# Full-height score products in an attention stage, and a GEMM stage's sums, differences and low halves moved from GpSimd to VectorE

## The chip, the cores and the metric

The kernel runs on one core of a Trainium2 chip. The metric is the device time of one execution, in microseconds (us); less is better. The core's engines run side by side, each through its own list of instructions in a fixed order: TensorE (PE in the profile; PEld is its weight loading), VectorE (DVE), ScalarE (ACT), GpSimd (POOL) and SyncE (SP), which issues most of the DMAs. An engine whose next instruction waits holds up everything behind it in its list.

## The reference, cut to what matters

One step of a one-layer encoder over 1,152 rows of 1,024 features (1,024 prompt rows and 8 times 16 sample rows). Three branches (a state space S5, a pooling branch, a cross-attention into 256 memory tokens) are gated, merged and multiplied by `w_out`; a residual and a gated feed-forward block follow.

```python
def memory_attention(q, mk, mv):                       # 4 heads of 64
    s = jnp.einsum('blhd,bmhd->bhlm', qh, mk) * (MEM_HEAD_DIM ** -0.5)
    p = jax.nn.softmax(s, axis=-1)
    o = jnp.einsum('bhlm,bmhd->blhd', p, mv)
...
    x = x + rmsnorm(merged @ p['w_out'], p['g_post1'])
    h2 = rmsnorm(x, p['g_pre2'])
    x = x + rmsnorm(ConvFFN(h2), p['g_post2'])         # up: 1024 -> 2 x 2816, down: 2816 -> 1024
```

## The kernel before, in words

Every large product is made in three passes from operands that are split into a high and a low part (`split`: ScalarE rounds the high part to fp32r, another engine subtracts it from the source; lines 63 and 64). `mm3` (lines 103, 106, 107) issues the three matmuls of one k-tile: high by high, high by low, low by high. The 1,152 rows lie in three chunks of 384 columns. The order of the instructions on each engine comes from a scheduler that works ahead of time from the code and a model of its own; `keep_in_program_order`, `issue_after` and `high_priority` pin a few of them.

**The attention** (lines 775 to 846, in phase 1). Queries, keys and values of the prompt come back from DRAM and are split into three tiles: `a0` holds the high queries (columns 0 to 2047) and the high and low keys, `a1` the low queries and, in four of its partitions, the negated row maxima `mT`, `a2` the values and the exponentials. Two heads share the 128 partitions: head `e` of a pair has partitions 64e to 64e+63. A first pass (line 811) makes scores from the high parts alone, rows by tokens, for the row maxima. A second pass (lines 835 to 838) makes the scores as tokens by rows: for each of 16 tiles (two row groups, two head pairs, two heads, two token halves) three products over 64 partitions and one over 4 partitions (`sel` by `mT`), which subtracts the maximum, each 512 columns wide. ScalarE takes the exponential (line 839), line 842 multiplies by the values, and VectorE divides (lines 843 and 844). Between these matmuls the scheduler lays the products of the gates (lines 103 to 107 with `hhi`, `hlo`), so TensorE has other work all through this stage.

**The output GEMM** (`phase_o`, lines 1023 to 1188). For chunk c and feature tile f, `out(c, f)` is 24 matmuls; ScalarE evacuates it (line 1078) and squares it (line 1053), and GpSimd adds the square to the chunk's sum `ssa` (line 1057). `sums` multiplies these sums by ones (line 1065, up to 18 matmuls of one column) for a root mean square, whose power runs on GpSimd (line 86); ScalarE makes three diagonal tiles of it (line 94), and TensorE spreads it over all rows (line 96). `resid` then scales the chunk, adds x (lines 1095 and 1099 on VectorE) and squares again, and `norm` scales for the second norm (line 1117). The steps of chunk c-1 are laid between the products of chunk c. At the end chunks 0 and 1 are combined for seven block products in place of eight (a Strassen scheme): VectorE and GpSimd form the blocks (lines 1153 and 1160 to 1165) and their splits (`bB..`, `bT..`). The feed-forward weights of the first two feature tiles (ff 0 and 1) are combined likewise in `up_w`: sums and differences S1 to S4 from lines 1232 to 1238, then their splits. `prods` issues the block products: for ff 0 the order is 1, 2, the sums of chunk 2, 6, 5, its `resid`, 7, 3, 4; for ff 1 it is 1, 2, the second sums of chunk 2, 6, 5, its `norm`, 7, 3, 4.

Buffers that set the order here: `w1` has six tiles and `w2` four, which hold first the split weights of the output GEMM and then those of `up_w`. So the high part of a new weight (line 63) waits until TensorE is done with the product that read the buffer.

Of the kernel before, what the change touches and what calls it, by code (L numbers as in the profile page):

```python
# [32 lines left out]
class K:  # L33
# [741 lines left out]
    def attention(self, P, pools):  # L775


        nc = self.nc
# [4 lines left out]
        Kh = a0[:, 2048:2560].rearrange("p (h m) -> p h m", h=2)  # L783
        Kl = a0[:, 2560:3072].rearrange("p (h m) -> p h m", h=2)
# [4 lines left out]
        self.split(Kh, Kl, r)  # L789
# [11 lines left out]
        sel = P.tile([4, 4, 128], F32R, tag="tg", name="sel")  # L801
        nc.vector.tensor_copy(sel, self.ident[0:4, 0:4, None].to_broadcast([4, 4, 128]))

        mx = P.tile([128, 8, 2, 2], F32, tag="mx", name="mx")
        mT = a1[0:4, 2048:3072].rearrange("p (j k) -> p j k", j=8)
        for j in range(8):
            sc = [self.sm().rearrange("p (h m) -> p h m", h=2) for _ in range(2)]
            for e in range(2):
                es = slice(64 * e, 64 * e + 64)
                for hp in range(2):  # L810
                    nc.tensor.matmul(sc[e][:, hp, :], Qh[es, hp, j, :], Kh[es, hp, :], start=True, stop=True)
                nc.vector.tensor_reduce(mx[:, j, e, :], sc[e], axis=AX.X, op=OP.max)
            if j == 3:
                next(dec)
        for g in range(2):
            t = self.sm()
            for j in range(4):
                nc.tensor.transpose(t[0:4, j * 128:j * 128 + 128], mx[:, 4 * g + j].rearrange("p e h -> p (e h)"), self.ident)
            nc.scalar.activation(mT[:, 4 * g:4 * g + 4], t[0:4].rearrange("p (j k) -> p j k", j=4), AF.Copy, scale=-1.0)
# [3 lines left out]
        for g in range(2):  # L823
            gs = slice(4 * g, 4 * g + 4)
            for hp in range(2):
                yt = P.tile([128, 4, 128], F32, tag="tmp", name="yt")
                yf = yt.rearrange("p j k -> p (j k)")
                for e in range(2):
                    es, zs = slice(64 * e, 64 * e + 64), slice(64 - 64 * e, 128 - 64 * e)
                    pT = a2[:, 1024 + 1024 * (n % 2):2048 + 1024 * (n % 2)].rearrange("p (m l) -> p m l", m=2)  # L830
                    n += 1
                    for m in range(2):
                        s = self.sm()
                        ms = slice(128 * m, 128 * m + 128)
                        nc.tensor.matmul(s, Kh[es, hp, ms], Qh[es, hp, gs], start=True, stop=False)
                        nc.tensor.matmul(s, Kh[es, hp, ms], Ql[es, hp, gs], start=False, stop=False)
                        nc.tensor.matmul(s, Kl[es, hp, ms], Qh[es, hp, gs], start=False, stop=False)
                        nc.tensor.matmul(s, sel[:, 2 * e + hp, :], mT[:, gs], start=False, stop=True)
                        nc.scalar.activation(pT[:, m, :], s, AF.Exp, scale=0.125)
                    o = self.sm()  # L840
                    for m in range(2):
                        nc.tensor.matmul(o, va[:, m, 2 * hp + e, :], pT[:, m, :], start=m == 0, stop=m == 1)  # L842
                    nc.vector.reciprocal(yf[es], o[zs])
                    nc.vector.tensor_mul(yf[es], o[es], yf[es])
# [178 lines left out]
    def phase_o(self):  # L1023
# [6 lines left out]
        if True:  # L1030
# [16 lines left out]
            def sumsq(f, src, ss, last=8):  # L1047
# [3 lines left out]
                else:  # L1051
# [4 lines left out]
                    else:  # L1056
                        self.sqadd = G.tensor_add(ss[0], ss[0], sq)  # L1057
# [74 lines left out]
            for c in range(3):  # L1132
                ss.append(ssa())
                for f in range(8):
# [4 lines left out]
                    if c:  # L1139
# [7 lines left out]
                        elif f == NF[c] + 1:  # L1147
                            with tc.high_priority():
                                norm(c - 1, rs)
                            if c == 1:  # L1150
                                op("B11", h0[:, lo])
                                op("B21", h0[:, up])
                                G.tensor_sub(h0[:, up], h0[:, up], h0[:, lo])
# [11 lines left out]
            G.tensor_sub(h0[:, up], h0[:, up], h1[:, lo])  # L1165
            op("T3", h1[:, lo], G)
            op("T4", h0[:, up], G)
# [12 lines left out]
            with tc.issue_after(self.diag.ins):  # L1180
                self.up_w(s1, (None, G, G, G))
# [32 lines left out]
    def up_w(self, s, eng=(None,) * 4):  # L1214

        G = self.nc.gpsimd
# [620 lines left out]
```

## Time and profile before

| | before |
|---|---|
| median of 3 runs | 1626.8 us (1624.13 to 1631.04) |
| the profiled execution's own time | 1622.7 us |
| its span, first to last instruction | 1620.9 us |
| TensorE busy in the span | 1558.3 us |
| VectorE, ScalarE, GpSimd busy | 1031.3, 586.2, 586.3 us |
| mean granted TensorE clock | 0.979 |

The span runs from the first to the last instruction; 1.8 us of the execution's time lie around it. Rows of the timeline read: start, duration, engine, line, operation, output<-input, partitions*columns of the weights, partitions x columns of the streamed operand, count, and in brackets the idle time before it with the engine that ended it. Ends of matmuls are modelled, so the distance from one start to the next says what a matmul costs. A row that merges several ("x3") gives the time of all of them.

### The profile page before, as it was taken

What the parts mean: (1) busy time and instruction counts of PE and PEld (TensorE: products, weight loads), DVE (VectorE), ACT (ScalarE), POOL (GpSimd) and SP (SyncE); (2) the same over time, 40 slices, a digit from 0 to 9 for tenths busy, and PEclk for the clock granted to TensorE, in tenths of its full rate; (3) what the DMA queues carried; (4) which work ended last, traced back from release to release, by engine and by line L of the source; (5) the groups of instructions that cost most, each with busy time, mean ns of one, the idle gap of its engine ahead of it and who ended that gap; (6) DMA issues with size and microseconds to landing.
All of it is one profiled execution on the core that took longest, in us unless ns stands there. A gap on an engine that the chain in (4) does not pass through costs nothing.

```text
span 1620.9 us, 22934 instructions
## 1 busy us (share of the span) xinstructions
PE 1558.3 (96%) x8964; PEld 1511.3 (93%) x8964; DVE 1031.3 (64%) x1549; ACT 586.2 (36%) x893; POOL 586.3 (36%) x509
## 2 busy tenths in 40 slices
PE   6899999999999999999879999999999999999996
PEld 5899999868899999998879999999999998999996
DVE  7864987645643354624678655555655658788866
ACT  6322444253321242434445333433333333332321
POOL 2400001000011143326666444534443426655546
PEclk9899999999999999999879999999999999999998
DMA  6343334413232235122323221212121233133214
GB/s 245 100 146 95 107 114 145 150 64 121 95 117 81 71 80 162 56 96 76 122 88 129 76 75 62 82 69 81 54 82 69 82 135 122 51 110 103 91 64 166
DMA packets 98460, 163.44 MB, mean 101 GB/s; under 512 B 23216, under 2 KB 68656, under 8 KB 98352
## 3 DMA queue, kind: packets, MB, share of 16 engines
q1 hardware_dynamic: 97920, 161.75, 30.3%
q8 instruction: 70, 1.15, 0.3%
q14 instruction: 38, 0.31, 0.1%
q10 hardware_dynamic: 432, 0.23, 0.0%
HBM read 119.52 MB, written 42.42 MB: 100 GB/s over the span
## 4 chain that ended last, share of the span: by engine, by line
PE 79%; DVE 9%; issue 3%; DMA 3%; ACT 2%; POOL 1%; POOLq 0%; SPq 0%; DVEq 0%; ACTq 0%
PE pc L107 14%; PE pc L103 14%; PE pc L106 14%; PE ps L103 10%; PE ps L106 10%; PE ps L107 10%; PE ps L842 1%; DVE dB L64 1%; DMA Ts<-DG 1%; POOL ssa L1057 1%; DVE wlo L64 1%; PE ps L1065 1%; DMA DG<-gs 1%; DMA dwr<-in_w_down 1%; DVE mg L1095 1%
## 5 line engine op out<-in xcount | busy, mean ns | idle before, releaser
L103 PE MATMUL pc<-hhi,whi 128*128 128x384 f32 x760 | 259.9, 342 | 7.7 <-ACT hhi L126 7.6
L106 PE MATMUL pc<-hlo,whi 128*128 128x384 f32 x760 | 260.7, 343 | 2.6 <-DVE hlo L127 2.6
L107 PE MATMUL pc<-hhi,wlo 128*128 128x384 f32 x760 | 257.7, 339 | 0.5 <-DVE wlo L64 0.5
L63 ACT ACTIVATE whi<-rawt 128x1024 fp32r<-128x1024 f32 x102 | 107.5, 1055 | 180.7 <-PE pc L106 80.7
L64 DVE TENSOR_TENSOR wlo<-rawt,whi 128x1024 fp32r<-128x1024 f32 x102 | 131.9, 1295 | 56.9 <-ACT whi L63 56.3
L103 PEld LDWEIGHTS pc<-hhi,whi 128*128 128x128 f32 x760 | 144.8, 191 | 10.3 <-ACT hhi L126 7.6
L106 PEld LDWEIGHTS pc<-hlo,whi 128*128 128x128 f32 x760 | 144.7, 190 | 7.4 <-DVE hlo L127 3.5
L107 PEld LDWEIGHTS pc<-hhi,wlo 128*128 128x128 f32 x760 | 144.6, 190 | 3.2 <-issue 1.6
L200 DVE TENSOR_TENSOR sg<-pc,rb 128x384 f32<-128x384 f32 x95 | 52.3, 553 | 122.7 <-PE pc L107 120.2
L107 PE MATMUL pc<-h2hi,wlo 128*128 128x384 f32 x352 | 119.1, 338 | 2.1 <-DVE wlo L64 2.0
L103 PE MATMUL pc<-h2hi,whi 128*128 128x384 f32 x352 | 118.3, 336 | 0.0
L106 PE MATMUL pc<-h2lo,whi 128*128 128x384 f32 x352 | 118.2, 336 | 0.0
L64 DVE TENSOR_TENSOR S<-S,S 128x512 fp32r<-128x512 f32 x85 | 75.9, 895 | 64.2 <-ACT S L63 62.2
L63 ACT ACTIVATE S<-S 128x512 fp32r<-128x512 f32 x88 | 55.1, 629 | 160.2 <-PE ps L107 89.8
L917 ACT ACTIVATE sg<-sg,vec 128x384 f32<-128x384 f32 x72 | 44.1, 613 | 148.2 <-DVE sg L200 121.2
L1004 POOL TENSOR_TENSOR mg<-mg,sgl 128x384 f32<-128x384 f32 x24 | 28.2, 1174 | 171.9 <-DVE sgl L1002 168.6
L103 PE MATMUL ps<-bT,S 128*128 128x384 f32 x240 | 80.2, 334 | 0.0
L106 PE MATMUL ps<-bT,S 128*128 128x384 f32 x240 | 80.2, 334 | 0.0
L107 PE MATMUL ps<-bT,S 128*128 128x384 f32 x240 | 80.2, 334 | 0.0
L1237 POOL TENSOR_TENSOR S<-rawt 128x512 f32<-128x512 f32 x22 | 29.8, 1355 | 125.9 <-PE ps L107 124.3
L63 ACT ACTIVATE dhi<-dwr 128x1024 fp32r<-128x1024 f32 x38 | 39.7, 1058 | 95.9 <-PE pc L106 61.4
L107 PEld LDWEIGHTS pc<-h2hi,wlo 128*128 128x128 f32 x352 | 66.1, 188 | 2.8 <-DVE wlo L64 2.8
(458 smaller groups left out, 4401.0 us busy)
## 6 DMA issues: line engine op xcount, KB each, us to landing
rawt<-in_w_up SPq DMA_DIRECT2D x48, 512.0 KB, 3.3
Dact<-t SPq DMA_DIRECT2D x22, 576.0 KB, 3.5
rawt<-in_w_gate SPq DMA_DIRECT2D x24, 512.0 KB, 3.5
dwr<-in_w_down SPq DMA_DIRECT2D x22, 512.0 KB, 3.5
Dsg<-sg SPq DMA_DIRECT2D x45, 192.0 KB, 1.9
sgl<-Dsg SPq DMA_DIRECT2D x45, 192.0 KB, 2.4
dBr<-Dact SPq DMA_DIRECT2D x8, 768.0 KB, 5.7
xT<-in_xT SPq DMA_DIRECT2D x12, 384.0 KB, 7.6
```

The source lines that it names most:

```text
L63: nc.scalar.activation(hi, src, AF.Copy)
L64: (eng or nc.vector).tensor_sub(lo, src, hi)
L103: i = nc.tensor.matmul(out, whi, xhi, start=start, stop=False)
L106: nc.tensor.matmul(out, whi, xlo, start=False, stop=False)
L107: nc.tensor.matmul(out, wlo, xhi, start=False, stop=stop)
L200: self.nc.vector.tensor_mul(sg, b, self.rb[:, c, :])
L842: nc.tensor.matmul(o, va[:, m, 2 * hp + e, :], pT[:, m, :], start=m == 0, stop=m == 1)
L917: self.nc.scalar.activation(sg, sg, AF.Sigmoid, bias=self.vec[:, V_BGATE + m:V_BGATE + m + 1])
L1004: nc.gpsimd.tensor_add(m, m, sp)
L1057: self.sqadd = G.tensor_add(ss[0], ss[0], sq)
L1065: m = nc.tensor.matmul(s3[:, t:t + 1], s[:, t * 128:t * 128 + 128], self.ones[:, 0:1], start=(i, t) == (0, 0), stop=(i, t) == (len(ss) - 1 ...
L1237: G.tensor_sub(s3, a11, a21)
```

## The change

In the attention the keys of each head get a tile of their own over all 128 partitions, with zeros in the other head's half (`Kh` and `Kl` with an index `e`; two memsets of 128x1024 on GpSimd, and the split in two halves of 64 partitions). The second pass then multiplies over 128 partitions; the queries of the other head meet zeros. `mT` becomes a tile of its own of 128 partitions, cleared once, and `sel` gets 128 partitions. The first pass still works on 64 partitions. In `phase_o` the additions of squares, the two block differences that GpSimd made, the low halves of T3 and T4, and in `up_w`, for ff 0 and 1, the sums and differences and the low halves of S2 to S4 go to VectorE. For ff 2 and above `up_w` is as before.

```diff
--- before.py
+++ after.py
@@ -775,18 +775,23 @@
     def attention(self, P, pools):


         nc = self.nc
         a0, a1 = [self.mtile([128, 3072], F32R, f"at{i}") for i in range(2)]
         a2 = self.mtile([128, 3072], F32, "at2")
         Qh = a0[:, 0:2048].rearrange("p (h j k) -> p h j k", h=2, j=8)
         Ql = a1[:, 0:2048].rearrange("p (h j k) -> p h j k", h=2, j=8)
-        Kh = a0[:, 2048:2560].rearrange("p (h m) -> p h m", h=2)
-        Kl = a0[:, 2560:3072].rearrange("p (h m) -> p h m", h=2)
+        Kh = a0[:, 2048:3072].rearrange("p (e h m) -> p e h m", e=2, h=2)
+        Kl = a1[:, 2048:3072].rearrange("p (e h m) -> p e h m", e=2, h=2)
         va = a2[:, 0:1024].rearrange("p (m h d) -> p m h d", m=2, h=4)
         dec = self.attention_decode(P)
         r = P.tile([128, 2, 256], F32, tag="tmp", name="kr")
         nc.sync.dma_start(r, self.O["mk"])
-        self.split(Kh, Kl, r)
+        nc.gpsimd.memset(a0[:, 2048:3072].bitcast(F32), 0.0)
+        nc.gpsimd.memset(a1[:, 2048:3072].bitcast(F32), 0.0)
+        for e in range(2):
+            es = slice(64 * e, 64 * e + 64)
+            self.split(Kh[es, e], Kl[es, e], r[es])
         for hp in range(2):
             r = P.tile([128, 8, 128], F32, tag="U", name="qr")
             nc.sync.dma_start(r, self.Dq[hp].rearrange("p (j k) -> p j k", j=8)[:, :, 0:128])
@@ -798,25 +803,27 @@
         vh = va.rearrange("p m (a e) d -> p m a e d", e=2)
         for e in range(2):
             nc.gpsimd.tensor_copy(vh[:, :, :, e, 64 * e:64 * e + 64], r[:, :, :, e, :])
-        sel = P.tile([4, 4, 128], F32R, tag="tg", name="sel")
-        nc.vector.tensor_copy(sel, self.ident[0:4, 0:4, None].to_broadcast([4, 4, 128]))
+        sel = P.tile([128, 4, 128], F32R, tag="tg", name="sel")
+        nc.vector.tensor_copy(sel, self.ident[:, 0:4, None].to_broadcast([128, 4, 128]))

         mx = P.tile([128, 8, 2, 2], F32, tag="mx", name="mx")
-        mT = a1[0:4, 2048:3072].rearrange("p (j k) -> p j k", j=8)
         for j in range(8):
             sc = [self.sm().rearrange("p (h m) -> p h m", h=2) for _ in range(2)]
             for e in range(2):
                 es = slice(64 * e, 64 * e + 64)
                 for hp in range(2):
-                    nc.tensor.matmul(sc[e][:, hp, :], Qh[es, hp, j, :], Kh[es, hp, :], start=True, stop=True)
+                    nc.tensor.matmul(sc[e][:, hp, :], Qh[es, hp, j, :], Kh[es, e, hp, :], start=True, stop=True)
                 nc.vector.tensor_reduce(mx[:, j, e, :], sc[e], axis=AX.X, op=OP.max)
             if j == 3:
                 next(dec)
+        mTt = P.tile([128, 1024], F32R, tag="CA", name="mT")
+        nc.gpsimd.memset(mTt.bitcast(F32), 0.0)
+        mT = mTt.rearrange("p (j k) -> p j k", j=8)
         for g in range(2):
             t = self.sm()
             for j in range(4):
                 nc.tensor.transpose(t[0:4, j * 128:j * 128 + 128], mx[:, 4 * g + j].rearrange("p e h -> p (e h)"), self.ident)
-            nc.scalar.activation(mT[:, 4 * g:4 * g + 4], t[0:4].rearrange("p (j k) -> p j k", j=4), AF.Copy, scale=-1.0)
+            nc.scalar.activation(mT[0:4, 4 * g:4 * g + 4], t[0:4].rearrange("p (j k) -> p j k", j=4), AF.Copy, scale=-1.0)
         next(dec)
         pools[0]()
         n = 0
@@ -832,9 +839,9 @@
                     for m in range(2):
                         s = self.sm()
                         ms = slice(128 * m, 128 * m + 128)
-                        nc.tensor.matmul(s, Kh[es, hp, ms], Qh[es, hp, gs], start=True, stop=False)
-                        nc.tensor.matmul(s, Kh[es, hp, ms], Ql[es, hp, gs], start=False, stop=False)
-                        nc.tensor.matmul(s, Kl[es, hp, ms], Qh[es, hp, gs], start=False, stop=False)
+                        nc.tensor.matmul(s, Kh[:, e, hp, ms], Qh[:, hp, gs], start=True, stop=False)
+                        nc.tensor.matmul(s, Kh[:, e, hp, ms], Ql[:, hp, gs], start=False, stop=False)
+                        nc.tensor.matmul(s, Kl[:, e, hp, ms], Qh[:, hp, gs], start=False, stop=False)
                         nc.tensor.matmul(s, sel[:, 2 * e + hp, :], mT[:, gs], start=False, stop=True)
                         nc.scalar.activation(pT[:, m, :], s, AF.Exp, scale=0.125)
                     o = self.sm()
@@ -1054,7 +1061,7 @@
                     if f >= last:
                         ss.append(sq)
                     else:
-                        self.sqadd = G.tensor_add(ss[0], ss[0], sq)
+                        self.sqadd = V.tensor_add(ss[0], ss[0], sq)
                         if self.pin_sq:
                             tc.keep_in_program_order(self.sqadd)

@@ -1150,7 +1157,7 @@
                             if c == 1:
                                 op("B11", h0[:, lo])
                                 op("B21", h0[:, up])
-                                G.tensor_sub(h0[:, up], h0[:, up], h0[:, lo])
+                                V.tensor_sub(h0[:, up], h0[:, up], h0[:, lo])
             wms.close()
             self.open_u()
             s0 = self.up_begin(0)
@@ -1162,9 +1169,9 @@
             V.tensor_sub(h1[:, up], h1[:, up], h0[:, lo])
             op("T2", h1[:, up])
             op("T1", h0[:, lo])
-            G.tensor_sub(h0[:, up], h0[:, up], h1[:, lo])
-            op("T3", h1[:, lo], G)
-            op("T4", h0[:, up], G)
+            V.tensor_sub(h0[:, up], h0[:, up], h1[:, lo])
+            op("T3", h1[:, lo])
+            op("T4", h0[:, up])
             self.raws[1] = self.up_raw(1)
             s1 = self.up_begin(1)

@@ -1178,7 +1185,7 @@
             with tc.high_priority():
                 ss2 = resid(2, rs)
             with tc.issue_after(self.diag.ins):
-                self.up_w(s1, (None, G, G, G))
+                self.up_w(s1)
             prods(s0, 7, 3, 4)
             prods(s1, 1, 2)
             rs = sums(ss2)
@@ -1213,7 +1220,7 @@

     def up_w(self, s, eng=(None,) * 4):

-        G = self.nc.gpsimd
+        G = self.nc.vector if s.ff < 2 else self.nc.gpsimd
         ra, rg = self.raws[s.ff]
         a11, a12, a21, a22 = ra[:, 0:4], ra[:, 4:8], rg[:, 0:4], rg[:, 4:8]
         s.aw = self.load_w(None, pool=self.w2, r=ra)
```

The instructions' order follows from the scheduler, so the places that matter are shown as they stand in the lists. First GpSimd's list at the seam of chunks 1 and 2 of the output GEMM, before; `rs_y` is the root mean square (line 86), `ssa` a sum of squares, S_ and `rawt` belong to `up_w`, `mg0` is chunk 0:

```order
L1057 TENSOR_TENSOR ssa_6581<-ssa_6581,sq_6903 128x384
L1232 TENSOR_TENSOR S_7251<-rawt_7028 128x512
L1153 TENSOR_TENSOR mg0_4074<-mg0_4074 128x1536
L86 TENSOR_TENSOR rs_y_6940<-rs_v_6938,mhalf_82 128x3
L1233 TENSOR_TENSOR S_7251<-S_7251,rawt_7026 128x512
```

The same engine with the change, from the last addition of the stage ahead:

```order
L984 TENSOR_TENSOR mg2_4082<-mg2_4082,sg_6212 128x384
L86 TENSOR_TENSOR rs_y_6621<-rs_v_6619,mhalf_82 128x3
L86 TENSOR_TENSOR rs_y_6831<-rs_v_6829,mhalf_82 128x3
L86 TENSOR_TENSOR rs_y_6946<-rs_v_6944,mhalf_82 128x3
L86 TENSOR_TENSOR rs_y_7135<-rs_v_7133,mhalf_82 128x3
```

The powers now stand alone in GpSimd's list; all that stood between them has gone to VectorE.

VectorE's list with the change, in the residual of chunk 1 (`mg1`), from its third addition of x; `sq_6992` to `sq_7018` are the five squares that the second sum of this chunk needs, and `wlo_7254`, `wlo_7276` are low weights of ff 0 (line 64), whose high part waits for `out(2, 3)` and `out(2, 4)`:

```order
L1064 TENSOR_TENSOR ssa_6983<-ssa_6983,sq_6992 128x384
L64 TENSOR_TENSOR wlo_7254<-rawt_7032,whi_7253 128x1024
L1064 TENSOR_TENSOR ssa_6983<-ssa_6983,sq_7002 128x384
L1106 TENSOR_TENSOR mg1_4081<-mg1_4081,x_7021 128x384 x2
L1064 TENSOR_TENSOR ssa_6983<-ssa_6983,sq_7005 128x384
L64 TENSOR_TENSOR wlo_7276<-rawt_7034,whi_7275 128x1024
L1064 TENSOR_TENSOR ssa_6983<-ssa_6983,sq_7015 128x384
L1064 TENSOR_TENSOR ssa_6983<-ssa_6983,sq_7018 128x384
```

Before, the additions were on GpSimd and these low weights came behind the last addition of x on VectorE; now they stand between the additions of squares, two of which follow the second low weight.

VectorE's list with the change, in the residual of chunk 2 (`mg2`), where `wlo_7658` is a low weight for the feed-forward stage whose buffer is free once product 2 of ff 1 is done:

```order
L1064 TENSOR_TENSOR ssa_7379<-ssa_7379,sq_7398 128x384
L64 TENSOR_TENSOR wlo_7658<-rawt_7653,whi_7657 128x1024
L1064 TENSOR_TENSOR ssa_7379<-ssa_7379,sq_7401 128x384
L1102 SCALAR_TENSOR_TENSOR mg2_4082<-mg2_4082,vec_72,ps_7377 128x384 x2
L1106 TENSOR_TENSOR mg2_4082<-mg2_4082,x_7404 128x384 x2
L1064 TENSOR_TENSOR ssa_7379<-ssa_7379,sq_7411 128x384
L1064 TENSOR_TENSOR ssa_7379<-ssa_7379,sq_7414 128x384
L1102 SCALAR_TENSOR_TENSOR mg2_4082<-mg2_4082,vec_72,ps_7377 128x384 x2
L1106 TENSOR_TENSOR mg2_4082<-mg2_4082,x_7417 128x384 x2
```

Before, the corresponding low weight (`wlo_7652`) stood behind the last addition of x of this chunk; now half of the residual stands behind it. TensorE's list differs between the two kernels only in how the gate products are laid between the attention's matmuls; from the middle of the next stage on it is the same.

## The prediction

> **What bounds the kernel now.** I read the page first, then the stretches by window, then what TensorE waited for, and last the timeline of each engine at the two changed places.
>
> ```profile
> PE 1558.3 (96%) x8964; PEld 1511.3 (93%) x8964; DVE 1031.3 (64%) x1549; ACT 586.2 (36%) x893; POOL 586.3 (36%) x509
> ...
> core 0: us, PE busy (x) PEld busy (x) DVE busy (x) ACT busy (x) POOL busy (x), PEclk, DMA share, GB/s
> 320.00:360.00 40.00, 40.00 (x176) 28.41 (x175) 17.95 (x18) 17.60 (x24) 0.23 (x2) 1.00 0.27 87
> 760.00:800.00 40.00, 34.97 (x168) 34.12 (x169) 25.85 (x33) 16.62 (x34) 22.80 (x17) 0.83 0.33 109
> 800.00:840.00 40.00, 27.92 (x136) 26.17 (x134) 35.17 (x28) 17.42 (x27) 30.11 (x17) 0.80 0.29 96
> ...
> 715.00:875.00 160.00, 139.26 (x727) 134.18 (x726) 105.37 (x120) 72.77 (x129) 94.85 (x69) 0.89 0.27 89
> ```
>
> TensorE is the bound: 96% busy. In the attention (320 to 360) it never idles, so there only cheaper matmuls help. At the output GEMM's seam (715 to 875) it idles 160 - 139.3 = 20.7 us and is granted 0.80 to 0.83 of its clock in the worst 80 us, while VectorE and GpSimd are both loaded. Two different limits, so two sums.
>
> ```profile
> PE ps L1065 <- POOL ssa L1057: 10.8, 4, 6.3
> ...
> PE pc L106 <- DVE bT L64: 3.7, 2, 3.0
> ```
>
> Named releasers at the seam (total us, waits, longest): GpSimd's sums of squares and VectorE's low halves; the diagonals, which follow GpSimd's power, come below.
>
> **Part one: the score products.** TensorE in the attention's second pass:
>
> ```profile
> 334.82 0.34 PE L103 MATMUL pc<-hhi,whi 128*128 128x384 f32 x1
> 335.09 0.49 PE L835 MATMUL ps<-at 64*128 64x512 f32 x1
> 335.43 0.39 PE L836 MATMUL ps<-at,at 64*128 64x512 f32 x1
> 335.66 0.39 PE L837 MATMUL ps<-at 64*128 64x512 f32 x1
> 335.98 0.50 PE L838 MATMUL ps<-at,sel 4*128 4x512 f32 x1
> 336.40 0.45 PE L106 MATMUL pc<-hlo,whi 128*128 128x384 f32 x1
> 336.69 0.34 PE L107 MATMUL pc<-hhi,wlo 128*128 128x384 f32 x1
> ...
> 349.43 0.34 PE L103 MATMUL pc<-hhi,whi 128*128 128x384 f32 x1
> 349.60 1.02 PE L842 MATMUL ps<-at 128*128 128x512 f32 x2
> ```
>
> From start to start a 384-column matmul costs 0.17 us between neighbours of 128 partitions (349.43 to 349.60, and that neighbour has 512 columns). Line 836 to 837, both on 64 partitions, is 0.23: the price of 512 columns without a change of height. Around every change of height there is more: L103 to L835 0.27 (+0.10), L835 to L836 0.34 (+0.11), L837 to L838 0.32 (+0.09), L838 to L106 0.42 (+0.19), L106 to L107 0.29 (+0.12). Sum 0.61 a group. With the change all these neighbours have 128 partitions, so each should cost what 128-partition neighbours cost. 16 groups by 0.61 are 9.8; in four places two groups touch and share an exit and an entry, so I take **-9.7**. Ends: 0 (the extra has another cause) and -11 (an eighth more, if the weight loads beside them gain as well).
>
> Edits that I cost at nothing:
>
> ```profile
> 279.39 0.95 POOL L797 MEMSET at<- 128x1024 f32 x1 [14.17 <-PE ps L629]
> ...
> 277.47 0.63 ACT L63 ACTIVATE at<-kr 128x512 fp32r<-128x512 f32 x1 [0.78 <-DMA kr<-out_mk]
> ```
>
> Three memsets of 0.95 on GpSimd, which had idled 14 us ahead of such a one; the keys' split in halves, at most 0.63 more on ScalarE and the like on VectorE; `sel` with more partitions but as many columns. The gate products cover them: TensorE has no idle time there. Without that cover the first scores would start some 0.95 + 0.63 = 1.6 later. The first pass keeps its 64 partitions and its cost.
>
> A rule of the Trainium skill speaks against this part ("TensorE: Matmul & The Clock Gate", Part 3, The mechanism): a weight load overlaps a running matmul only when it goes to another row group, so equal heights would expose every load.
>
> ```profile
> L103 PEld LDWEIGHTS pc<-hhi,whi 128*128 128x128 f32 x760 | 144.8, 191 | 10.3 <-ACT hhi L126 7.6
> ```
>
> By this row a load takes 0.19; were it exposed for 64 products, that is 12.2 in place of the 9.7, a loss of 2.5. But neighbours of 128 partitions follow at 0.17, less than the load alone. The trace disagrees with that rule here, and I keep it as a small rival.
>
> **Part two: the seam, in order of time.**
>
> ```profile
> 755.30 3.49 POOL L1153 TENSOR_TENSOR mg<-mg 128x1536 f32<-128x1536 f32 x1
> 758.75 0.86 POOL L86 TENSOR_TENSOR rs_y<-rs_v,mhalf 128x3 f32<-128x3 f32 x1
> ...
> 758.95 0.34 PE L107 MATMUL pc<-mhi,wlo 128*128 128x384 f32 x1
> 761.30 0.91 PE L96 MATMUL ps<-diag,ones 128*128 128x384 f32 x2 [2.01 <-ACT diag L94]
> 762.48 0.52 PE L107 MATMUL pc<-mhi,wlo 128*128 128x384 f32 x1
> ...
> 765.36 0.49 PE L107 MATMUL pc<-mhi,wlo 128*128 128x384 f32 x1
> ```
>
> (a) The power (line 86) stands behind a block difference of 3.49. That one leaves GpSimd, as do the additions between. With the power at 755.3 in its place it ends at 756.2, and the diagonals, which came 1.7 behind it (759.6 to 761.3), are there at 757.9, before TensorE asks for them at 759.1. The block difference itself goes to VectorE, which idles most of the time between the norm and the residual there. 758.95 to 761.30 is 2.35 where 0.17 would do: -2.2. Behind the idle time ten matmuls run at half clock (762.48 to 765.36 holds nine steps of 0.32): -1.5. Two short waits for `ssa`, the rest of the 10.8 in the wait row beside the 3.73 and 6.31 below, lose some -0.5. Sum **-4.2**.
>
> ```profile
> 779.99 1.44 PE L1065 MATMUL ps<-ones,ssa 128*128 128x1 f32 x6 [3.73 <-POOL ssa L1057]
> ...
> L63 ACT ACTIVATE whi<-rawt 128x1024 fp32r<-128x1024 f32 x10 | 10.5, 1049 | 5.7 <-PE pc L106 5.7
> 857.15 1.21 DVE L64 TENSOR_TENSOR wlo<-rawt,whi 128x1024 fp32r<-128x1024 f32 x1
> 769.40 1.48 DVE L1099 TENSOR_TENSOR mg<-mg,x 128x384 f32<-128x384 f32 x3
> ```
>
> (b) The second sum of chunk 1 waits 3.73 for GpSimd's additions. On VectorE an addition costs 0.5 (1.48 for three), but the last two stand behind `wlo_7276`, whose high part waits for `out(2, 4)`, the very product that TensorE ends before this sum: 1.05 + 1.21 + 2 x 0.5 and some 0.3 of handing over give 3.5. A new wait in the old one's place, with the same slow clock behind it: **0**.
>
> ```profile
> 791.59 4.29 DVE L1117 SCALAR_TENSOR_TENSOR mg<-mg,vec,ps 128x384 f32<-128x384 f32 x8 [8.55 <-PE ps L96]
> ...
> 805.25 8.30 DVE L64 TENSOR_TENSOR bT<-mg,bT 128x1536 fp32r<-128x1536 f32 x2 [0.55 <-ACT bT L63]
> L64 DVE TENSOR_TENSOR bB<-mg,bB 128x1536 fp32r<-128x1536 f32 x3 | 5.3, 1756 | 0.2
> ```
>
> (c) T2's low half. Before: 13.7 from the norm's start to 805.25, then 4.15, stretched, where the same size takes 1.76 when GpSimd is quiet: 17.8. After, with GpSimd nearly empty: 4.3 for the norm, six operations of 1.76 (the moved difference among them), two additions and an evacuation at 0.5: 16.4. So the wait of 3.0 falls by 1.0 to 1.4, and I take 1.0, since T2's high half on ScalarE comes first and was not stretched; T1 follows after 1.76 rather than 4.15 and its wait of 0.7 goes. **-2.0**.
>
> ```profile
> 820.43 0.34 PE L103 MATMUL pc<-bT,whi 128*128 128x384 f32 x1
> 822.84 0.45 PE L106 MATMUL pc<-bT,whi 128*128 128x384 f32 x1 [2.08 <-POOL bT L64]
> 823.89 0.52 PE L103 MATMUL pc<-bT,whi 128*128 128x384 f32 x1
> ...
> 826.77 0.51 PE L103 MATMUL pc<-bB,whi 128*128 128x384 f32 x1
> ```
>
> (d) Product 4 waited for T4's low half from GpSimd. On VectorE there stand between T2's low half and the end of T4's: T1, T3 and T4 by 1.76, a low weight by 1.21, an evacuation and S2's low half by 0.5 to 0.7, together 7.7. TensorE has products 6, 5, 7 and 3 to do in that time, 48 matmuls by 0.17, the spread of a mean by some 0.7 and a slow stretch by 1.5, together 10.4. So T4 is ready about 2.5 ahead; the wait (820.43 to 822.84, 2.2 too long) goes, and with it the ten slow matmuls from 823.89 (nine steps of 0.32) and their 1.5: **-3.7**. If that margin is eaten, 0 to 2 of it come back.
>
> ```profile
> 830.42 0.34 PE L107 MATMUL pc<-bB,wlo 128*128 128x384 f32 x1
> 837.07 1.44 PE L1065 MATMUL ps<-ones,ssa 128*128 128x1 f32 x6 [6.31 <-POOL ssa L1057]
> 840.93 0.67 PE L103 MATMUL pc<-bT,S 128*128 128x384 f32 x1
> ```
>
> (e) Chunk 2's second sum. Product 2 of ff 1 ends at 830.6 (830.42 + 0.17); the next product starts at 840.93, 10.3 later. After, `wlo_7658` waits for that product 2, and behind it on VectorE stand three additions of squares, four scalings and four additions of x, all of which the sum needs: 1.05 + 1.21 + 3 x 0.5 + 4 x 0.54 + 4 x 0.5, then two squares and the sum's columns (some 3): 11.1. **+0.8**, and from both sides: -6 (no queue) to +5 (stretched as now).
>
> The additions of squares outside this stretch fall where VectorE waits for `out(c, f)` and cost nothing; if one stood ahead of a norm, it would cost its 0.5. No DMA is added; on SyncE's list a few loads of `w_up` and x change places by two or three rows, which I cost at nothing, from -1 to +2 for a load that lands later.
>
> Sum of the seam: -4.2 + 0 - 2.0 - 3.7 + 0.8 = -9.1. With -9.7 that is -18.8. The profiled execution took 1622.7, so 1603.9; the median of the runs shown lies 4.1 above that execution, and I go half of that way: **1605.9**.
>
> **Rivals.** *The seam closes:* VectorE keeps ahead and the waits in (b), (c) and (e) mostly go too, up to the 20.7 idle: 1622.7 - 9.7 - 20 = 1593, against it the lists' two low weights. *The seam gives nothing:* each wait moves from GpSimd to VectorE's single list: 1613. For it: VectorE is already busy 35.2 of 40 us before 840. *The heights give nothing,* or expose the loads: 1613.6 to 1616. Against it: the 0.17. *Slower:* VectorE's stretched durations (4.15 against 1.76) come from its own traffic, not from GpSimd's. Then (b), (c) and (e) grow by some 6 each: +18 - 9.7 gives 1631; it loses as soon as each grows by over 3.2. Against it: stretched rows stand only where GpSimd works.
>
> **Numbers.** Forecast 0.60 (own range 1599 to 1612), the seam closes 0.14, the seam gives nothing 0.15, the heights give nothing 0.06, slower 0.05. Less than 0.5% (8 us) can hardly be told from no change. The first two and most of the third are faster by more; the rest of the middle ones lie about the bound. So 0.87, 0.09, 0.04. The range 1594 to 1617 leaves out the lowest of the second case and the last.
>
> **What would show it.** Lines 842 to 845 (835 to 838 before) at 0.23 from start to start, with 0.17 at their edges, and TensorE still without idle time there; no wait at line 96 by diagonals; 1536-column operations on VectorE at 1.76; no wait of product 4; waits of line 1072 (1065 before) that end with VectorE, 3.5 and 8 to 9 us long. It is wrong if the groups stay at 0.3 and 0.4, or if VectorE is the releaser of more than 20 us of TensorE's idle time.

## The result, and the profile after

The changed kernel takes 1606.4 us (median of 4 runs, 1605.3 to 1608.3) beside 1625.5 for the kernel before (median of 4, 1624.1 to 1631.0): a ratio of 0.988, interval 0.985 to 0.990. The prediction was 1605.9, with 1594 to 1617 as its range. The profiled execution has a span of 1605.3 and a time of 1607.1, 15.6 less than the 1622.7 of before, where the sum of the prediction was 18.8 less.

First the page's engine shares and the stretches by window, as before (PE, PEld, DVE, ACT, POOL busy, granted clock):

```profile
PE 1546.5 (96%) x8964; PEld 1512.9 (94%) x8964; DVE 1044.1 (65%) x1602; ACT 586.4 (37%) x894; POOL 510.8 (32%) x460
...
320.00:360.00 40.00, 40.00 (x201) 33.71 (x200) 21.91 (x24) 18.10 (x25) 0.23 (x2) 1.00 0.31 106
760.00:800.00 40.00, 34.34 (x170) 33.53 (x169) 30.74 (x39) 19.22 (x34) 2.96 (x4) 0.81 0.36 124
800.00:840.00 40.00, 32.74 (x165) 31.83 (x165) 31.03 (x54) 17.45 (x32) 5.37 (x5) 0.85 0.26 89
715.00:875.00 160.00, 144.52 (x773) 140.97 (x772) 123.98 (x176) 76.17 (x132) 31.98 (x32) 0.91 0.30 104
```

In the attention TensorE is as full as before, but 201 matmuls fit into the 40 us that held 176. At the seam GpSimd falls from 94.9 to 32.0 us and VectorE rises from 105.4 to 124.0; TensorE still idles 160 - 144.5 = 15.5 us there, 5.2 less. (The windows are the same times and not quite the same work: at the first column sum the changed kernel is 6.9 ahead.) The waits of TensorE between 715 and 875 (total us, times, longest):

```profile
PE ps L1072 <- DVE ssa L1064: 10.9, 3, 6.6
...
PE pc L106 <- DVE bT L64: 1.8, 1, 1.8
```

The rows for the diagonals and for `bT` from GpSimd are gone. The sums wait as long as before (10.9 against 10.8), now for VectorE. The score products, in the timeline of TensorE and of its weight loads:

```profile
336.37 0.39 PE L842 MATMUL ps<-at 128*128 128x512 f32 x1
...
336.60 0.40 PE L843 MATMUL ps<-at,at 128*128 128x512 f32 x1
...
336.83 0.40 PE L844 MATMUL ps<-at,at 128*128 128x512 f32 x1
336.83 0.19 PEld L845 LDWEIGHTS ps<-mT,sel 128*128 128x128 f32 x1
337.06 0.40 PE L845 MATMUL ps<-mT,sel 128*128 128x512 f32 x1
337.07 0.19 PEld L107 LDWEIGHTS pc<-hhi,wlo 128*128 128x128 f32 x1
337.30 0.34 PE L107 MATMUL pc<-hhi,wlo 128*128 128x384 f32 x1
337.30 0.19 PEld L103 LDWEIGHTS pc<-hhi,whi 128*128 128x128 f32 x1
```

All four start 0.23 apart, the price of 512 columns and nothing else, and each load of 0.19 (336.83 for line 845, 337.07 for line 107) lies beside the matmul ahead of it.

One number per part is best read as the time between two starts of the same matmul in two traces. The table has, for each kernel run here, the start of the attention's first score product against before; the time from there to the first column sum (437.74 before); from there to the first product behind the row broadcast of chunk 2's norm (130.04 before, 717.00 to 847.04); and the rest to the last matmul. Positive is later or longer.

```
                      start of     attention to   seam     rest
                      attention    first sum
changed kernel          +2.99         -9.87       -8.56   -0.16
e1_att                  +1.03        -10.64       +1.03   +1.33
e2_seam                 +2.03         -0.05       -8.55   -0.19
e3_pass1                -0.16        -15.46       -8.63   +0.39
e4_four                 -0.48         -3.37       -9.67   -0.25
f1_s5                   +0.15        -10.35       -9.71   -0.91
f2_low                  -0.33         -9.19       -5.06   +1.13
f4_a                    +0.36         -1.44       -6.67   +0.97
f3_both                 +0.88        -14.28       -5.39   +1.13
g1_wg                   -2.22        -10.43       -9.42   +0.31
g2_best                 +0.33        -16.33       -9.29   -0.84
g4_wg2                  +1.75        -14.51      -11.82   +2.89
```

The first column is no effect of the change: it runs from -2.2 to +3.0 among kernels that compute the same up to there, and +2.0 in one whose attention isn't touched. The others scatter as well: the changed kernel, e2_seam, e3_pass1 and e4_four have the same seam and lie between -8.55 and -9.67, and five kernels with one attention between -9.19 and -10.64. So a difference of 2 us in a column, and 3 to 4 us in a whole time, can be the scatter of one execution.

### The profile page after: what moved, and what is told of

Same layout as the page of the kernel before. It is cut to its first block, busy times and chain, and to the rows that moved or that the text cites. A ratio compares the mean times of both kernels' runs of the same rounds, so it can differ in the third digit from the quotient of the medians.

```text
span 1605.3 us, 22914 instructions
## 1 busy us (share of the span) xinstructions
PE 1546.5 (96%) x8964; PEld 1512.9 (94%) x8964; DVE 1044.1 (65%) x1602; ACT 586.4 (37%) x894; POOL 510.8 (32%) x460
## 3 DMA queue, kind: packets, MB, share of 16 engines
q8 instruction: 70, 1.15, 0.3%
## 4 chain that ended last, share of the span: by engine, by line
PE 80%; DVE 9%; DMA 3%; issue 2%; ACT 2%; POOL 1%; POOLq 0%; SPq 0%; DVEq 0%; ACTq 0%
PE pc L107 15%; PE pc L103 15%; PE pc L106 14%; PE ps L103 11%; PE ps L106 11%; PE ps L107 11%; DMA Ts<-DG 1%; PE ps L849 1%; DMA DG<-gs 1%; DVE wlo L64 1%; DVE Xs L598 1%; PE ps L1072 1%; DVE mg L1124 1%; PE ps L763 0%; DVE sg L200 0%
## 5 line engine op out<-in xcount | busy, mean ns | idle before, releaser
L64 DVE TENSOR_TENSOR wlo<-rawt,whi 128x1024 fp32r<-128x1024 f32 x102 | 128.5, 1262 | 56.2 <-ACT whi L63 55.8
L64 DVE TENSOR_TENSOR S<-S,S 128x512 fp32r<-128x512 f32 x88 | 72.5, 826 | 56.2 <-ACT S L63 54.2
```

The lines of the kernel that those rows point to most:

```text
L64: (eng or nc.vector).tensor_sub(lo, src, hi)
```

## The experiments

**Each part alone, and the rule of equal heights.** Four kernels: before with the attention's part; before with the rest of the change; the changed kernel with its first pass on 128 rows too; and the changed kernel with one of the four score products back on 4 rows.

```diff
--- e3_pass1
-nc.tensor.matmul(sc[e][:, hp, :], Qh[es, hp, j, :], Kh[es, e, hp, :], start=True, stop=True)
+nc.tensor.matmul(sc[e][:, hp, :], Qh[:, hp, j, :], Kh[:, e, hp, :], start=True, stop=True)
--- e4_four
-nc.tensor.matmul(s, sel[:, 2 * e + hp, :], mT[:, gs], start=False, stop=True)
+nc.tensor.matmul(s, sel[0:4, 2 * e + hp, :], mT[0:4, gs], start=False, stop=True)
```

> The kernel before with the attention's part of the change alone. Theory (each change of height between neighbouring products costs 0.1 to 0.2 us, 0.61 for a group of four, 16 groups, and the two parts don't touch): 9.7 us less than before, some 1616 beside a before of 1625.5; the four score products 0.23 apart and 0.17 at their edges; the seam as before, with 10 to 11 us of waiting for GpSimd's ssa. Rival (the parts need each other, because the earlier end of the attention also moves the seam against its loads and clock): under 6 us less, or over 14. Rival (the 3.0 us that the changed kernel is later at the attention's first score product, 282.25 against 279.26, are brought by the new split of the keys and the memsets): this kernel starts its first score product at 281 to 283 too; if they are the chance of one execution, at 279 to 280.

> The kernel before with the output GEMM's part alone; the attention keeps 64-row and 4-row score products. Theory (the power came late behind a 3.5 us block difference, T2's low half was stretched by GpSimd's work, T4's low half came late from GpSimd): 8.6 to 9.1 us less than before, some 1616.5; the waits at the sums end with VectorE's ssa, 3.8 and 6.6 us long; no wait for the diagonals and none for T4. Rival (VectorE's longer list costs as much as GpSimd's late halves did, and the whole gain is the attention's): within 2 us of before. The sum of both parts should be 17 to 19 us.

> The changed kernel, with the first pass (the row maxima, 32 products of 256 columns) on 128 rows too: the keys are already padded with zeros. Theory of the heights: a visit of these products now costs 0.10 at its entry, 0.20 at its exit and 0.11 after it, 0.41 in all, on top of 0.115 for each 256 columns; 16 to 17 visits, so 6.5 us less at most, and 5 if a product of 256 columns can't follow its weight load in less than 0.19. So 1600 to 1601.5 beside 1606.4. Rival (the gain of the second pass came from the longer product chain or from the other operand tiles and not from equal heights): within 1 us of the changed kernel.

> The changed kernel, with the last of the four score products (line 845) back on 4 rows. Theory of the heights: this product alone brings back an entry of 0.09 to 0.10, an exit of 0.19 and 0.12 after it wherever another product follows: 0.40 a group, 16 groups, 6.4 us more than the changed kernel, 1612 to 1613; lines 842 to 844 stay 0.23 apart. Rival (64 rows were slow and 4 rows cost nothing of their own): as the changed kernel, within 1.5 us. Rival (the exit is paid once for a whole group, whatever stands in it): 0.3 a group, 4.8 us.

Measured: e1_att 1615.6, e2_seam 1615.0, e3_pass1 1602.9, e4_four 1608.9 (one run), beside a before of 1626.6. By the medians the parts give 11.0 and 11.7, against 20.3 for the whole change from the same before (19.2 from its own): they add within the scatter. The table says it more sharply: each leaves the other's column alone (-10.64 and +1.03; -0.05 and -8.55). e1_att's seam still waits for GpSimd.

e4_four loses 9.87 - 3.37 = 6.5 us of the attention, where 6.4 was expected, and e3_pass1 gains 15.46 - 9.87 = 5.6 more. (Their whole times, 1608.9 and 1602.9, miss the 1612 to 1613 and the 1600 to 1601.5 expected by 3.1 and 1.4, no more than whole times scatter.) Their rows of TensorE, e4_four first, then e3_pass1:

```profile
340.39 0.39 PE L843 MATMUL ps<-at,at 128*128 128x512 f32 x1
340.62 0.40 PE L844 MATMUL ps<-at,at 128*128 128x512 f32 x1
340.95 0.49 PE L845 MATMUL ps<-mT,sel 4*128 4x512 f32 x1
341.37 0.44 PE L107 MATMUL pc<-hhi,wlo 128*128 128x384 f32 x1
341.65 0.34 PE L103 MATMUL pc<-hhi,whi 128*128 128x384 f32 x1
```

```profile
306.19 0.33 PE L103 MATMUL pc<-hhi,whi 128*128 128x384 f32 x1
306.37 0.40 PE L815 MATMUL ps<-at 128*128 128x256 f32 x2
306.60 0.34 PE L106 MATMUL pc<-hlo,whi 128*128 128x384 f32 x1
306.78 0.33 PE L107 MATMUL pc<-hhi,wlo 128*128 128x384 f32 x1
```

In e4_four only the steps at the 4-row product are long: 0.33 into it (340.62 to 340.95), 0.42 out of it, 0.28 behind it, against 0.23, 0.23 and 0.17. 0.10 + 0.19 + 0.11 is 0.40 for one visit, and 16 of them are 6.4. In e3_pass1 two products of 256 columns take 0.23 together, with 0.18 on either side; in the changed kernel such a visit cost 0.41 more. So the price belongs to the change of height: neither to 64 rows as such, nor to the operands. The Trainium skill states it as a drain ("TensorEngine Tiling (Array Packing)", Key Properties): changing the tiling mode, not just the tile, drains TensorE. These rows agree and give it its size here. The rule of the Trainium skill that the prediction weighed ("TensorE: Matmul & The Clock Gate", Part 3, The mechanism) would have exposed the loads; the 0.19 loads under steps of 0.23 and 0.17 above disagree with it.

**Who pays at the seam.** The second group keeps the changed kernel and gives GpSimd work back (f1_s5: the second up block's S5 operands; f2_low: the low halves of the first two up blocks' weights; f3_both: these two and the first pass), or makes only the first half of the seam's change (f4_a).

```diff
--- f1_s5
-        G = self.nc.vector if s.ff < 2 else self.nc.gpsimd
+        G = self.nc.vector if s.ff < 1 else self.nc.gpsimd
-                self.up_w(s1)
+                self.up_w(s1, (None, G, G, G))
--- f2_low
-        s.aw = self.load_w(None, pool=self.w2, r=ra)
+        s.aw = self.load_w(None, pool=self.w2, r=ra, eng=self.nc.gpsimd if s.ff < 2 else None)
-        s.gw = self.load_w(None, pool=self.w2, r=self.raws[s.ff][1])
+        s.gw = self.load_w(None, pool=self.w2, r=self.raws[s.ff][1], eng=self.nc.gpsimd if s.ff < 2 else None)
--- f4_a (against before)
-                        self.sqadd = G.tensor_add(ss[0], ss[0], sq)
+                        self.sqadd = V.tensor_add(ss[0], ss[0], sq)
-                                G.tensor_sub(h0[:, up], h0[:, up], h0[:, lo])
+                                V.tensor_sub(h0[:, up], h0[:, up], h0[:, lo])
```

> The changed kernel, with the second up block's S5 operands (two sums, two differences, three low halves) back on GpSimd, whose list is nearly empty there now. Theory of the list (the second sum of chunk 2 waits for as much work as stands on VectorE's list between the end of T4 and the last squares; five operations of 0.6 to 0.69, 3.1 us, leave it): the stretch from product 2's last matmul to the next product falls from 11.6 to 8.5, and the kernel is 3 us faster, 1603.5. Rival of the shared stretch (two-operand work of GpSimd makes VectorE's own operations longer, as the 4.15 beside 1.76 in the kernel before suggests): GpSimd works some 9 us in the same 15 us, VectorE's 1536-, 1024- and 384-column operations there grow by 20 to 100%, and the stretch stays at 11 to 15. Which it is, the mean duration of VectorE's additions of x and low halves in that stretch tells: 0.51 and 1.75 if GpSimd doesn't matter.

> The changed kernel, with the low halves of the first two up blocks' weights (four operations of 1.21 on VectorE, two ahead of each second sum) on GpSimd. Theory (the low weights queued ahead are what makes the new waits of 3.8 and 6.6 us): the wait at chunk 1's second sum falls by 2.3 to 1.5, that at chunk 2's by 1.2 to 2.4, with some slow clock less, 3.5 to 5 us in all, 1601.5 to 1603. Rival (the waits are set by the chain product, copy, square, addition, and the queue is only what fills it): under 1 us at each. Rival of the shared stretch: each low half takes GpSimd 2.7 us or more and makes VectorE's operations beside it as much longer, so no gain or up to 3 us lost.

> The kernel before with only the additions of squares and the block difference of line 1153 on VectorE; the differences and low halves of T3 and T4 and all S5 operands stay on GpSimd. By the steps of the prediction (a) alone comes: 4.2 to 4.5 us by the second sum of chunk 1 (the power no longer stands behind the block difference, no wait for the diagonals), (b) 0 within 1, and the waits for T2 (3.0) and T4 (2.1) stay as they were, since GpSimd still stretches T2's low half (4.15, not 1.75) and makes T4's. Then 4.5 us less than before at T4, and 2 to 6 in all by what the second sum of chunk 2 does. Rival (the power was late for another reason, such as the sums themselves): the wait for the diagonals stays. Rival (taking the squares off GpSimd alone brings T4 early enough): the wait for T4 goes too, 7 to 8 us less than before.

> The changed kernel with all three: first pass on 128 rows, the second up block's S5 operands and the four low weights on GpSimd. If the list of VectorE is what the sums wait for and GpSimd doesn't slow it: 5.6 from the first pass (as measured in its own run), 3 from the operands and 3.5 to 5 from the low weights, 12 to 13 in all, 1593 to 1595. If GpSimd's work stretches VectorE's as much as it relieves it: the first pass alone, 1600 to 1602. If GpSimd, with some 20 us of work in the stretch, is late with a half that a product needs: waits for GpSimd come back, 1602 to 1606.

Measured: f1_s5 1603.4, f2_low 1609.3, f4_a 1618.3, f3_both 1605.7, beside a before of 1625.4.

f2_low tells most. It took four operations of 1.21 off VectorE, and the seam became 3.5 us longer (-5.06 against -8.56). The wait at chunk 1's second sum, 3.8 before the edit, and the rows of GpSimd and VectorE ahead of it:

```profile
768.42 1.41 PE L1072 MATMUL ps<-ones,ssa 128*128 128x1 f32 x6 [6.15 <-DVE ssa L1064]
...
759.36 3.60 POOL L64 TENSOR_TENSOR wlo<-rawt,whi 128x1024 fp32r<-128x1024 f32 x1 [11.88 <-ACT whi L63]
763.26 2.34 POOL L64 TENSOR_TENSOR wlo<-rawt,whi 128x1024 fp32r<-128x1024 f32 x1 [0.31 <-ACT whi L63]
...
760.15 3.22 DVE L1064 TENSOR_TENSOR ssa<-ssa,sq 128x384 f32<-128x384 f32 x2
763.29 3.19 DVE L1106 TENSOR_TENSOR mg<-mg,x 128x384 f32<-128x384 f32 x2
766.41 3.69 DVE L1064 TENSOR_TENSOR ssa<-ssa,sq 128x384 f32<-128x384 f32 x6
```

Two additions take 1.0 when GpSimd is quiet. Beside GpSimd's operation of 2.34 two take 3.19: they lost 2.2, nearly all of that operation. Beside the one of 3.60 they lost as much, and that one took 1.3 longer than its sister. So it is no sharing of a rate: one engine stands while the other's operation runs. The Trainium skill says so too ("SBUF — State Buffer", Who interferes with whom): a VectorE instruction with two SBUF inputs and a GpSimd instruction that reads SBUF contend for an exclusive lock. Offloading a VectorE operation of 1.21 to GpSimd at 2.3 therefore costs VectorE about 1 us where both are busy.

f1_s5 shows half of the 3 expected at the seam: the wait at chunk 2's second sum fell from 6.63 to 5.08, not to 3.5. (Its column is lower by 1.15, and e4_four's is by 1.1 with no edit at the seam; so that its whole time meets the 1603.5 expected is in part scatter.) One pair of additions pays there:

```profile
802.23 2.95 DVE L1106 TENSOR_TENSOR mg<-mg,x 128x384 f32<-128x384 f32 x2
...
801.91 1.28 POOL L1244 TENSOR_TENSOR S<-rawt 128x512 f32<-128x512 f32 x1
803.15 1.61 POOL L1245 TENSOR_TENSOR S<-rawt,S 128x512 f32<-128x512 f32 x1
```

f3_both gained 4.4 in the attention, by the first pass, and lost 3.2 of it at the seam (-5.39, like f2_low). Its 1605.7 is level with the changed kernel's 1606.4, and misses the 1600 to 1602 of the case that GpSimd's work costs VectorE as much as it relieves it. It lies in the range of the third case, but for another reason: only 0.7 of TensorE's waits at the seam is for GpSimd.

f4_a is before with the squares and one block difference moved. Its waits:

```profile
PE ps L1065 <- DVE ssa L1057: 10.9, 3, 7.1
PE pc L106 <- DVE bT L64: 4.3, 2, 3.0
...
PE ps L96 <- ACT diag L94: 0.8, 1, 0.8
```

The wait for the diagonals fell from 2.0 to 0.8 and not to nothing: with the block difference gone, the power stands behind S5 sums on GpSimd. Up to chunk 1's second sum f4_a gained 3.4 of the changed kernel's 4.5. T2's wait of 3.0 stayed, as expected: its low half is still stretched. But there is no row for `bT` from GpSimd any more: T4's low half is still made by GpSimd and now comes in time, as the rival said, and the whole time is 7.1 less than before (7 to 8 by the rival, 2 to 6 without it). The squares are not the direct reason, though. GpSimd's rows, before first, then f4_a:

```profile
815.87 1.29 POOL L1237 TENSOR_TENSOR S<-rawt 128x512 f32<-128x512 f32 x1 [1.60 <-PE pc L107]
817.11 1.29 POOL L1238 TENSOR_TENSOR S<-rawt,S 128x512 f32<-128x512 f32 x1
818.35 4.43 POOL L64 TENSOR_TENSOR bT<-mg,bT 128x1536 fp32r<-128x1536 f32 x1
```

```profile
808.09 3.50 POOL L64 TENSOR_TENSOR bT<-mg,bT 128x1536 fp32r<-128x1536 f32 x1
811.55 2.27 POOL L1237 TENSOR_TENSOR S<-rawt 128x512 f32<-128x512 f32 x1
```

Before, ScalarE had T4's high half done at 813.5, but the low half stood behind two S5 operations in GpSimd's list and started at 818.35; no square is near. In f4_a the scheduler laid it ahead of them, and it ends 2.9 before the product that reads it (814.47). So its place in the list had made it late. The rest of the change adds 8.56 - 6.67 = 1.9, about what a column scatters.

**The low weights ahead of the sums.** g1_wg moves a low weight without giving it to GpSimd: it is issued behind the norm's diagonals. g4_wg2 does so for both up blocks on top of g2_best, which joins the first pass on 128 rows and f1_s5.

```diff
--- g1_wg
         op("S4", s4, eng[3])
-        self.up_wg(s)
+        if s.ff:
+            self.up_wg(s)
...
             self.up_w(s0)
+            with tc.issue_after(self.diag.ins):
+                self.up_wg(s0)
```

> The changed kernel, with the second split of the first up block's weights (a high half of 1.05 on ScalarE, a low half of 1.21 on VectorE) issued only behind the diagonals of chunk 1's norm: the low half leaves the list ahead of that chunk's second sum and GpSimd gets nothing. Theory (b) of the prediction (the new wait of 3.8 us is VectorE's list, with this low half in it): the wait falls by 1.2, to 2.6, or by up to 2.2 if the high half on ScalarE was ahead of a square too; the wait of 6.6 at chunk 2 stays; 1 to 2 us in all, 1604 to 1605.5. Rival (the wait is the chain of product, copy, square and addition, and the low half only fills it): the wait stays within 0.3 of 3.8.

> The changed kernel with the two edits that gained by themselves: the first pass on 128 rows (5.6 us between the attention's first score product and the first sum) and the second up block's S5 operands on GpSimd (1.9 us at the seam). They lie 400 us apart and should add: 7.5 us less than the changed kernel, 1598 to 1600. If they don't add, 1600 to 1603.

> As the run before, and both up blocks' second weight splits behind the diagonals of the norms, which takes one low half of 1.21 from the list ahead of chunk 1's second sum and two ahead of chunk 2's. If those lists are what the sums wait for: 7.5 and 1.2 and 2.4 more, 11 us less than the changed kernel, 1594 to 1597, with waits of some 2.6 and 2.7 at the two sums. Rival (the low halves, now queued ahead of chunk 2's norm, make the norm and its halves late for the products behind, and a wait for h2lo or for product 4's weight takes over): 1597 to 1600, with a new row of waiting for VectorE behind the norm.

Measured: g1_wg 1605.4, g2_best 1598.5 (ratio to before 0.983, 0.981 to 0.986), g4_wg2 1598.7 (0.984, 0.981 to 0.986), beside a before of 1625.1. In g1_wg the wait at chunk 1's second sum fell from 3.82 to 2.98, two thirds of the low half's 1.21, and the other stayed, at 6.27. So the list is part of that wait, and most of the rest is the sum's own work on VectorE. In g4_wg2 both waits fell:

```profile
PE ps L1072 <- DVE ssa L1064: 6.8, 3, 3.4
...
PE ps L1072 <- ACT sq L1060: 1.2, 1, 1.2
PE pc L103 <- ACT bT L63: 0.6, 1, 0.6
PE pc L106 <- DVE h2lo L64: 0.3, 1, 0.3
```

By the table its seam is 3.3 us shorter than the changed kernel's, with 0.6 and 0.3 of new waits for halves that the low weights now delay. Its whole time misses the 1594 to 1597 expected and lies where its rival said, that low halves late for later products take the gain: 0.9 of such waits is there, and in the profiled execution a later stretch was longer too (the last column). Whether g4_wg2 is better than g2_best is therefore open; both beat the changed kernel by some 8 us.

## Why the prediction held, point by point

| step | predicted | measured, and where |
|---|---|---|
| part one, score products | -9.7 | -9.87 from the first score product to the first sum |
| (a) power behind the block difference | -4.2 | -4.47 to the last product ahead of chunk 1's second sum |
| (b) low weight ahead of that sum | 0 | -0.11 to the products behind it; a wait of 3.82 (3.5 predicted, 3.73 before) |
| (c) T2 and T1 | -2.0 | -1.40 to the products 6 and 5 |
| (d) T4 | -3.7 | -3.93 to the end of product 2 of ff 1 |
| (e) chunk 2's second sum | +0.8 | +1.35 |
| seam | -9.1 | -8.56 |
| ahead of the attention | 0 | +2.99, scatter |

**Part one** held by its mechanism and its size; e4_four and e3_pass1 show both directions. The keys' split and the memsets, costed at nothing, were covered: e1_att starts its scores at +1.0, e4_four at -0.5.

**(a)** held: the diagonals' wait is gone. f4_a adds a condition that I did not name: the S5 sums must leave GpSimd too, or 0.8 of that wait stays.

**(b)** held in place and size, and in part by its reason. The row of VectorE that the prediction named stands where it said (the second low weight here), and the one ahead of it wasn't charged:

```profile
763.27 1.21 DVE L64 TENSOR_TENSOR wlo<-rawt,whi 128x1024 fp32r<-128x1024 f32 x1
...
764.90 1.03 DVE L1106 TENSOR_TENSOR mg<-mg,x 128x384 f32<-128x384 f32 x2
...
766.31 1.22 DVE L64 TENSOR_TENSOR wlo<-rawt,whi 128x1024 fp32r<-128x1024 f32 x1
767.45 3.08 DVE L1064 TENSOR_TENSOR ssa<-ssa,sq 128x384 f32<-128x384 f32 x5
```

Without the second, the prediction's terms would leave a wait of 3.5 - 1.05 - 1.21 = 1.3. g1_wg takes it away, and 2.98 stay: the additions of x and of squares behind TensorE's last product set most of the wait by themselves. That the size was right is therefore partly luck.

**(c)** was too high by 0.6. The wait for T2 fell as predicted (2.97 to 1.84) and T1's went, but the slow clock behind it ran 16 steps of 0.32 where before it ran 10: a term that I had not given this step.

**(d)** held in its sum: on VectorE T4's low half ends 3.4 ahead of the product that reads it, at 804.3 (2.5 predicted). The move was enough, but not needed: f4_a leaves it on GpSimd, ahead of the S5 operations, and the wait goes as well. The prediction didn't see that it stood behind them.

**(e)** was too low by 0.5 (its terms add up to 10.9 and not to the 11.1 written, which makes it a little more): the wait is 6.63 where before it was 6.31, and 0.63 more passes inside the sum, for a square from ScalarE, the row `L1060` of the waits.

**Slower** (VectorE's stretch is its own) fell by this group of VectorE between 715 and 875, which had 4.19 as its mean before:

```profile
L64 DVE TENSOR_TENSOR bT<-mg,bT 128x1536 fp32r<-128x1536 f32 x4 | 6.8, 1750 | 0.0
```

With GpSimd quiet all are 1.75. **The heights give nothing** is out by e1_att, **the seam gives nothing** by e2_seam, **the seam closes** by the 10.9 of waits that are left. That the total came so near (1606.4 for 1605.9) is partly luck: the sum gave 1603.9 for the profiled execution, which took 1607.1, 3.0 of it ahead of the attention; and the 2.0 added on the way to the median rested on a median of before that fell by 1.3 as a run was added.

## What to carry to other kernels

On a TensorE that never idles, look at the steps from start to start around each odd-shaped matmul: a product of fewer rows between full ones costs 0.4 to 0.6 us beside its columns here, and zeros in the unused rows take that away. Moving work between VectorE and GpSimd is not a matter of adding it to the emptier list: where both have two-input work in the same microseconds, one stood here, so a shared stretch gains by giving all of it to the faster engine, up to the point where that engine's list becomes the wait. What is left after that is order: what isn't needed by the next sum goes behind it, and T4's low half was late by its place in a list.

## What the hardware showed that I had not expected

The slow clock behind a wait doesn't follow from the wait's length. Eleven of the thirteen traces have a wait of 2.0 to 2.1 us for a low weight behind the seam. In ten of them no slow step (0.32 from start to start for 384 columns, where 0.17 is usual) follows within 9 us, as in g2_best (first rows); only g4_wg2 (second rows) has some. TensorE:

```profile
848.05 0.44 PE L107 MATMUL pc<-h2hi,wlo 128*128 128x384 f32 x1 [2.04 <-DVE wlo L64]
848.33 0.34 PE L103 MATMUL pc<-h2hi,whi 128*128 128x384 f32 x1
848.50 0.34 PE L106 MATMUL pc<-h2lo,whi 128*128 128x384 f32 x1
```

```profile
849.27 0.44 PE L107 MATMUL pc<-h2hi,wlo 128*128 128x384 f32 x1 [2.10 <-DVE wlo L64]
...
850.53 0.52 PE L107 MATMUL pc<-h2hi,wlo 128*128 128x384 f32 x1
850.85 0.52 PE L103 MATMUL pc<-h2hi,whi 128*128 128x384 f32 x1
```

The first goes on at steps of 0.17; the second falls to steps of 0.32 one us later, and loses 1.6 us. In the trace of before a wait of 2.08 (for T4) is followed by such steps and this one, of 2.01, by none. The same code behind the same wait can differ too. The first six columns of chunk 1's second sum, in the changed kernel and then in e4_four:

```profile
768.74 1.41 PE L1072 MATMUL ps<-ones,ssa 128*128 128x1 f32 x6 [3.82 <-DVE ssa L1064]
```

```profile
771.79 0.80 PE L1072 MATMUL ps<-ones,ssa 128*128 128x1 f32 x6 [3.85 <-DVE ssa L1064]
```

With the columns behind them that makes the 1.1 by which e4_four's seam is shorter. The Trainium skill ("TensorE: Matmul & The Clock Gate", What's actually happening) describes the clock's monitor as a free-running window of some 3.4 us. If so, it would matter where a wait falls in the window, and these rows fit that; no run here shows the window itself, and it is longer than the waits of 2 us. So the price of 1.5 for slow clock behind a wait, as the prediction charged it, is no constant: behind waits of 1.8 to 2.1 us the traces have from no slow step to some 16 of them, 2.4 us.
